# Reordering two places of a one-layer encoder kernel: two high halves on ScalarE, and the last products of the MLP

## The chip, the cores and the metric

The kernel runs on one core of one Trainium2 chip. The metric is the device time of one execution in microseconds; the median of several executions is compared. A profiled execution gives one trace with the start and the length of every instruction.

## The reference

One layer on 512 positions of width 1024, all in float32: a combined input projection into forgetting attention and a gated linear recurrence, an output projection, cross attention to 256 memory tokens, and a squared-ReLU MLP of width 4096, each with a residual addition, then a final RMS norm.

```python
h = h + jnp.concatenate([fox_out, rec], axis=-1) @ w_out[l]
h = h + memory_cross_attention(rmsnorm(h, norm_x_g[l]), mem_n, w_xq[l], w_xkv[l], w_xo[l])
u = rmsnorm(h, norm_ff_g[l]) @ w1[l]
h = h + jnp.square(jax.nn.relu(u)) @ w2[l]
...
return rmsnorm(h, final_norm_g)
```

The change touches the last three of these lines: the start of `@ w1`, the end of `@ w2`, and the final norm with the store of the output.

## The kernel before

**Numbers in two halves.** Every float32 operand of a matrix product is split in a high half, rounded on ScalarE (ACT) by an `activation` with `Copy`, and a low half, the difference, made on VectorE (DVE). A product is three matmuls: high by high, high by low, low by high. `split_of` makes the halves of a weight tile (L179 the high one, L183 the low one; tiles `whu`, `wlu` for the first MLP matrix, `whd`, `wld` for the second). `whp` and `wlp`, the pools of weight halves, have four buffers each.

**Seven products.** Each MLP product of 2 by 2 blocks is done with seven block products instead of eight, named "1" to "7", on sums and differences of blocks. The hidden width is cut into eight groups of 512 (`NG` is 8). For each group `mlp_up7` does the seven products with the first matrix (L1473 to L1475), into PSUM banks U, V and Y, and `mlp_down` the seven with the second (L1629 to L1631). The last two groups, 6 and 7, are taken through `mlp_down` together, as one pair: each product runs over both groups and over two row halves `t`, in four blocks of six matmuls, accumulated in one PSUM bank for each `t`.

**Queues.** PE's order is the program's. On ACT and DVE a scheduler orders the instructions by priority and by its own clock, except within `tc.manual_schedule`, where their order among themselves is as written. All engines run their queues in order. A dependency with `NoSync` is an order on one engine alone.

**Ahead of the first group.** The last column chunk of the cross attention's output projection (`xw`, L253 to L255) is still on PE when ACT and DVE prepare the operands of the first group within a manual stretch (from L1798). `x_hi_of(n)` writes the high half `xs_hi` of the moving operand of product n (L1538), `x_lo_of(n)` the low half `xs_lo` (L1549 for product 6, L1551 for others), `x_dif` their source `xd` (L1523), `x_scaled` scales a chunk (`xg`, L1508), and `split_first("6", "h")` and `("6", "l")` are the two halves of product 6's weights. The tile `xs_hi` and the weight buffer that product 6's high half gets by rotation were both last read by L254.

**The closing pair.** `PRODUCTS` gives the order 1, 5, 6, 2, 7, 3, 4. `hidden_part` makes the two halves `hb` of the hidden operand (L1576 on ACT, L1580 and L1582 on DVE), some products ahead. `add_to` (L1595, L1597) adds a finished bank to rows of the accumulator: `acc[0..3]` are four blocks of 128 positions by 1024 columns, with the residual in them. Product 7 ends the right half of blocks 2 and 3, product 2 the left and product 3 the right half of blocks 0 and 1, product 4 the left half of blocks 2 and 3. `finish` does, when the first half of a block is done, its sum of squares `fe` (ACT, then POOL, L1749 and L1750) and its product with the gain, `fa` (POOL, L1752); for the second half of blocks 0 and 1 it only notes the block in `deferred`. After product 7, `onto_rows` adds the accumulator's left halves of blocks 2 and 3 and bank U together (L1654 to L1657), so that product 4 accumulates onto them.

`last_product` does product 4 in three parts: row half 0 in bank U (`u0`, L1672), then the left and the right quarter of row half 1 (`z0`, `z1`). Between and behind them stand, in written order, the sums of squares, the row scales (`row_scale`, a power on POOL, L1720), the two scalings of each block (`scale_a` on ACT, L1728, of the half already multiplied by the gain; `scale_b` on DVE, L1737) and the stores to the output (L1694, L1701, L1712 and L1732). Blocks 0 and 1 have their squares, scalings and stores within product 4. The scaling `scale_a` of block 2 stands behind the square of `z1` on ACT.

Of the kernel before, what the change touches and what calls it, by code (L numbers as in the profile page):

```python
# [13 lines left out]
ALU = mybir.AluOpType  # L14
# [32 lines left out]
def emit(  # L47
# [49 lines left out]
    def s4(shape, name, dt=F32):  # L97
        return s4p.tile([P] + shape, dt, tag="s4", name=name)
# [18 lines left out]
    def mm(name, shape=(S,)):  # L117
        return mmp.tile([P] + list(shape), F32, tag="mm", name=name)
# [10 lines left out]
    def f(a):  # L129
        return a.bitcast(F32)  # L130
# [1184 lines left out]
    sqs, comb, hbs = {}, {}, {}  # L1315
    PRODUCTS = ("1", "5", "6", "2", "7", "3", "4")
    SPLITS = ("1", "6", "5", "2", "7", "3", "4")
    FIRST = ("1", "2", "5", "6", "7", "3", "4")
    QUAD = {"1": "00", "2": "10", "3": "11"}
    raw_n = [0]  # L1320
# [96 lines left out]
            add_unit(("u", g, part), [UK, WT])  # L1417

    def down_units(gs):
        for name in PRODUCTS:  # L1420
            for g in gs:
                add_unit(("d", g, name), [2, S])

# [137 lines left out]
        comb[g] = {"1": A1a, "5": s5, "6": n6, "3": s3, "7": s7, "2": A1b, "4": A2b}  # L1561

    hb_order = [(g, name) for g in range(NG - 2) for name in PRODUCTS]
    hb_order += [(g, name) for name in PRODUCTS for g in (NG - 2, NG - 1)]
    hb_used = [0]

    def behind_w4(at, n):
        order_only = mybir.DependencyInfo(mybir.DependencyClass.NoSync, mybir.DependencyReason.DATA)
# [2 lines left out]
    def hidden_part(g, name):  # L1571

        src = comb[g][name]
        hb = s4([2, 2, HS], f"hb{g}{name}", R)
        sign = -1.0 if name == "6" else 1.0
        at = ac.activation(hb[:, 0], src, AF.Copy, scale=sign)  # L1576
        if g == 0 and name == "1":
            behind_w4(at, 0)
        if name == "6":
            ve.scalar_tensor_tensor(hb[:, 1], src, -1.0, f(hb[:, 0]), op0=ALU.mult, op1=ALU.subtract)  # L1580
        else:
            ve.tensor_tensor(hb[:, 1], src, f(hb[:, 0]), ALU.subtract)  # L1582
        hbs[g, name] = hb

    def hidden_ahead(key, n, within=None):
# [6 lines left out]
    def add_to(ps, rows, half, t, sign):  # L1592
        a = acc[2 * rows + t][:, half * S : (half + 1) * S]
        if sign > 0:
            ve.tensor_tensor(a, ps, a, ALU.add)  # L1595
        else:
            ve.scalar_tensor_tensor(a, ps, -1.0, a, op0=ALU.mult, op1=ALU.add)  # L1597

    PLAN = {
        "1": ("U", True, ()),  # L1600
# [8 lines left out]
    def mlp_down(gs):  # L1609

        end = gs[-1] == NG - 1
        banks = {}
        for n, name in enumerate(PRODUCTS):
            bank, first_, goes = PLAN[name]
            if end and name == PRODUCTS[-1]:
                last_product(gs, banks)
                return
            for g, t in [(g, t) for g in gs for t in range(2)]:
                whi, wlo = unit("d", g, name)
                hidden_ahead((g, name), 1)  # L1620
                hb = hbs[g, name]
                if first_ and g == gs[0]:
                    banks[bank, t] = {"U": sc, "Y": tr}[bank](f"{bank}{g}{t}")
                ps = banks[bank, t]
                ts_ = slice(t * P, (t + 1) * P)
                for k in range(2):
                    hi, lo = hb[:, 0, k, ts_], hb[:, 1, k, ts_]
# [3 lines left out]
                    at = te.matmul(ps, lo, whi[:, k, :], start=False, stop=k == 1, skip_group_check=True)  # L1631
                presum.tick(6 * S / 2400, at)
                if end and (g, t) == (gs[0], 1):
                    hidden_ahead((g, name), HB + 1)
                if g != gs[-1]:
                    continue
                if name == "1":
                    banks["V", t] = mm(f"V{g}{t}")
                    ac.activation(banks["V", t], ps, AF.Copy)
                for rows, half, sign in goes:  # L1640
                    add_to(ps, rows, half, t, sign)
                    if end and (name, rows) in FINAL:
                        finish(2 * rows + t, half)
            if end and name == "7":
                onto_rows(banks)
            hidden_ahead((gs[-1], name), HB, gs)
            yield

    onto = []

    def onto_rows(banks):

        u0, u1, a = banks["U", 0], banks["U", 1], acc[3]
        ve.tensor_tensor(u0, u0, acc[2][:, 0:S], ALU.add)  # L1654
        onto.append(mm("Z1")[:, 0:HS])
        ve.tensor_tensor(onto[0], u1[:, HS:S], a[:, HS:S], ALU.add)
        ve.tensor_tensor(a[:, 0:HS], u1[:, 0:HS], a[:, 0:HS], ALU.add)  # L1657

    def last_product(gs, banks):

        name = PRODUCTS[-1]

        def steps(g, t, cols):
            (whi, wlo), hb = unit("d", g, name), hbs[g, name]
            for k in range(2):
                hi, lo = (hb[:, x, k, t * P : (t + 1) * P] for x in range(2))
                yield from ((hi, whi[:, k, cols]), (hi, wlo[:, k, cols]), (lo, whi[:, k, cols]))

        def product(ps, t, cols, start):
            ops = [op for g in gs for op in steps(g, t, cols)]  # L1670
            for i, (a, b) in enumerate(ops):
                te.matmul(ps, a, b, start=start and i == 0, stop=i == len(ops) - 1, skip_group_check=True)  # L1672

        with tc.manual_schedule(engines={mybir.EngineType.Activation, mybir.EngineType.DVE}):
            u0 = banks["U", 0]
            product(u0, 0, slice(0, S), False)
            o2, o3 = s4([D], "fo2"), s4([D], "fo3")
            (half, o0, r0_), (_, o1, r1_) = deferred
            hs = slice(half * S, (half + 1) * S)
            e0 = sm(1, "fv0")  # L1680
            ac.activation(o0[:, hs], acc[0][:, hs], AF.Square, scale=1.0 / 32.0, accum_out=e0)
            gp.tensor_tensor(e0, e0, fin[0][0], op=ALU.add)
            row_scale(r0_, e0)
            row_scale(r1_, squares(acc[1][:, hs], o1[:, hs], fin[1][0], "fv1"))
            e2, e3, r2_, r3_ = sm(1, "fv2"), sm(1, "fv3"), sm(1, "fr2"), sm(1, "fr3")
            scale_b(0, half, o0, r0_)
            ac.activation(o2[:, 0:S], u0, AF.Square, scale=1.0 / 32.0, accum_out=e2)
            gp.tensor_tensor(e2, e2, fin[2][0], op=ALU.add)
            row_scale(r2_, e2)
            scale_a(0, o0, r0_)  # L1690
            scale_a(1, o1, r1_)
            scale_b(1, half, o1, r1_)
            for tb, o in ((0, o0), (1, o1)):
                nc.sync.dma_start(out[rows_(tb), :], o)  # L1694
            h0, h1 = slice(0, HS), slice(HS, S)
            z0, z1 = mm("Z0")[:, 0:HS], onto[0]
            product(z0, 1, h0, True)
            ve.tensor_tensor(acc[3][:, h0], z0, acc[3][:, h0], ALU.add)
            v3 = squares(acc[3][:, h0], o3[:, h0], fin[3][0], "fv30")
# [3 lines left out]
            ac.activation(o3[:, h1], z1, AF.Square, scale=1.0 / 32.0, accum_out=e3)  # L1703
            scale_a(2, o2, r2_)
            dma_a(nc.sync, 2, o2)
            ve.tensor_tensor(e3, e3, v3, ALU.add)
            row_scale(r3_, e3)
            scale_a(3, o3, r3_)
            dma_a(ac, 3, o3)
            for cs, src in ((h0, acc[3][:, h0]), (h1, z1)):  # L1710
                ve.scalar_tensor_tensor(o3[:, cs], src, r3_, gfin[0][:, cs], op0=ALU.mult, op1=ALU.mult)
            nc.sync.dma_start(out[rows_(3), 0:S], o3[:, 0:S])  # L1712

# [5 lines left out]
    def row_scale(r, v):  # L1719
        gp.tensor_tensor(r, v, mhalf[:, 0:1], op=ALU.pow)  # L1720
        return r
# [12 lines left out]
    def scale_b(tb, half, o, r, src=None):  # L1734
        cs = slice(half * S, (half + 1) * S)
        src = acc[tb][:, cs] if src is None else src
        ve.scalar_tensor_tensor(o[:, cs], src, r, gfin[half], op0=ALU.mult, op1=ALU.mult)  # L1737


    FINAL = (("2", 0), ("7", 1), ("3", 0))  # L1740
# [2 lines left out]
    def finish(tb, half):  # L1743
# [3 lines left out]
        if tb not in fin:  # L1747
# [4 lines left out]
            gp.tensor_tensor(ag, a[:, cs], gfin[half], op=ALU.mult)  # L1752
            fin[tb] = (e, cs, ag)
            return
        o, r = s4([D], f"fo{tb}"), sm(1, f"fr{tb}")
        deferred.append((half, o, r))

    for part in FIRST:
# [146 lines left out]
```

## Time and profile before

| | us |
|---|---|
| median of 3 runs | 753.86 (753.45 to 754.28) |
| profiled execution, its time | 753.76 |
| its span, first instruction to last | 751.8 |
| PE busy / weight loads / DVE / ACT / POOL | 743.0 / 652.7 / 544.6 / 440.7 / 202.3 |
| mean granted TensorE clock | 0.998 of full speed |
| the first MLP group starts on PE | 430.02 |
| the pair's product 7 starts | 728.85 |
| product 3 starts | 734.29 |
| product 4 starts | 739.73 |
| last matmul starts | 745.21 |

A row of a timeline has the start from the span's first instruction, the length, engine, line and operation, the tiles written and read with their sizes, the count of instructions merged into it, and in brackets how long the engine had been idle before and what ended that. A row of waits has who waited, for whom, the total in us, the times and the longest.

### The profile page before, as it was taken

Reading aid. Unit: us, or ns where it says so; the run is one execution under the profiler, and the core shown is the slowest. Engines: PE = TensorE matmul, PEld = TensorE weight load, DVE = VectorE, ACT = ScalarE, POOL = GpSimd, SP = SyncE. Lnnn points to the kernel's source line nnn. Section 1 sums busy time; section 2 is a strip of 40 time slices with the busy share of each in tenths; the row PEclk is TensorE's granted clock in tenths of the full one; section 3 lists DMA queues with packets and bytes.
Section 4 is the critical chain, followed back from the end, with each engine's and each line's share of the span. In section 5 each row is a group of like instructions: output and inputs, shape, how many; then the busy total and the mean of one; then the engine's idle time right before and its main releaser. Section 6 shows DMA issues by size and latency. Waiting matters only on the chain.

```text
span 751.8 us, 12385 instructions
## 1 busy us (share of the span) xinstructions
PE 743.0 (99%) x4645; PEld 652.7 (87%) x4645; DVE 544.6 (72%) x859; ACT 440.7 (59%) x735; POOL 202.3 (27%) x279
## 2 busy tenths in 40 slices
PE   9999999999999999999999999999999999999996
PEld 6889888888888988888888899898989899999985
DVE  5647873677878756645555799978787887878796
ACT  5655555655666532334434589766566757574863
POOL 7207531233433227621111212111111111100034
PEclk9999999999999999999999999999999999999999
DMA  8641987567957789986578799998989898977452
GB/s 249 200 116 58 307 263 224 182 223 258 294 183 224 261 223 210 196 165 123 121 168 191 118 246 230 245 218 243 239 219 233 221 252 212 243 190 231 134 112 112
DMA packets 109677, 152.92 MB, mean 203 GB/s; under 512 B 6145, under 2 KB 75818, under 8 KB 109618
## 3 DMA queue, kind: packets, MB, share of 16 engines
q1 hardware_dynamic: 85458, 112.52, 45.9%
q0 software_dynamic: 24000, 39.35, 30.3%
q8 instruction: 36, 0.59, 0.3%
q10 hardware_dynamic: 160, 0.27, 0.1%
q14 instruction: 23, 0.19, 0.1%
HBM read 147.91 MB, written 51.40 MB: 265 GB/s over the span
## 4 chain that ended last, share of the span: by engine, by line
PE 91%; DVE 4%; ACT 2%; issue 1%; POOL 1%; DMA 1%; POOLq 0%; SPq 0%; DVEq 0%; ACTq 0%
PE uU L1474 4%; PE uU L1475 4%; PE uU L1473 4%; PE U L1629 3%; PE U L1630 3%; PE U L1631 3%; PE xq L253 2%; PE wo L253 2%; PE xq L254 2%; PE xq L255 2%; PE xw L253 2%; PE xw L254 2%; PE wo L255 2%; PE wo L254 2%; PE uY L1475 2%; PE uY L1474 2%
## 5 line engine op out<-in xcount | busy, mean ns | idle before, releaser
L183 DVE TENSOR_TENSOR wlu<-wru,whu 128x1024 fp32r<-128x1024 f32 x53 | 64.0, 1226 | 26.3 <-ACT whu L179 26.2
L179 ACT ACTIVATE whu<-wru 128x1024 fp32r<-128x1024 f32 x53 | 55.7, 1058 | 41.2 <-PE U L1631 16.8
L183 DVE TENSOR_TENSOR wld<-wrd,whd 128x1024 fp32r<-128x1024 f32 x56 | 69.1, 1236 | 13.8 <-ACT whd L179 13.6
L179 ACT ACTIVATE whd<-wrd 128x1024 fp32r<-128x1024 f32 x56 | 59.0, 1053 | 14.0 <-PE uU L1474 6.3
L1629 PE MATMUL U<-whd,hb 128*128 128x512 f32 x120 | 46.8, 390 | 0.0
L1630 PE MATMUL U<-wld,hb 128*128 128x512 f32 x120 | 46.8, 390 | 0.0
L1631 PE MATMUL U<-whd,hb 128*128 128x512 f32 x120 | 46.7, 389 | 0.0
L1014 POOL TENSOR_SCALAR bi<-nF,Ft 128x128 f32<-128x128 f32 (+3 forms) x32 | 20.8, 656 | 60.4 <-PE pt L1046 33.8
L1474 PE MATMUL uU<-xs_lo,whu 128*128 128x256 f32 x128 | 36.3, 284 | 0.2 <-DVE xs_lo L1549 0.2
L1473 PE MATMUL uU<-xs_hi,whu 128*128 128x256 f32 x128 | 36.3, 284 | 0.0
L1475 PE MATMUL uU<-x_hi,wlu 128*128 128x256 f32 x128 | 36.2, 283 | 0.0
L1473 PE MATMUL uY<-xs_hi,whu 128*128 128x256 f32 x128 | 36.2, 283 | 0.0
L1474 PE MATMUL uY<-xs_lo,whu 128*128 128x256 f32 x128 | 36.2, 283 | 0.0
L1475 PE MATMUL uY<-xs_hi,wlu 128*128 128x256 f32 x128 | 36.2, 283 | 0.0
L1474 PE MATMUL uU<-x_lo,whu 128*128 128x256 f32 x128 | 36.2, 283 | 0.0
L1475 PE MATMUL uU<-xs_hi,wlu 128*128 128x256 f32 x128 | 36.2, 283 | 0.0
L1473 PE MATMUL uU<-x_hi,whu 128*128 128x256 f32 x128 | 36.2, 283 | 0.0
L444 POOL DMA_DIRECT2D wsd<-in_w_dram x16 | 17.8, 1116 | 63.7 <-PE xw L255 12.8
L1369 POOL DMA_DIRECT2D wrd<-in_w_dram x8 | 9.8, 1220 | 86.9 <-DVE wld L183 76.4
L444 POOL DMA_DIRECT2D wsu<-in_w_dram x14 | 17.1, 1220 | 48.2 <-PE xw L255 15.6
L1631 PEld LDWEIGHTS U<-whd,hb 128*128 128x128 f32 x120 | 22.5, 188 | 4.8
L1629 PEld LDWEIGHTS U<-whd,hb 128*128 128x128 f32 x120 | 22.6, 188 | 4.5
(958 smaller groups left out, 2621.2 us busy)
## 6 DMA issues: line engine op xcount, KB each, us to landing
wru<-in_w_dram SPq DMA_DIRECT2D x25, 512.0 KB, 8.0
wsd<-in_w_dram SPq DMA_DIRECT2D x24, 512.0 KB, 7.0
wrd<-in_w_dram SPq DMA_DIRECT2D x24, 512.0 KB, 4.4
wrd<-wsd SPq DMA_DIRECT2D x24, 512.0 KB, 6.0
wsu<-in_w_dram SPq DMA_DIRECT2D x21, 512.0 KB, 6.8
wru<-wsu SPq DMA_DIRECT2D x21, 512.0 KB, 5.8
wsd<-in_w_dram POOLq DMA_DIRECT2D x16, 512.0 KB, 6.6
wsu<-in_w_dram POOLq DMA_DIRECT2D x14, 512.0 KB, 7.1
```

The source lines that it names most:

```text
L179: at = ac.activation(hi, raw, AF.Copy)
L183: at_lo = ve.tensor_tensor(lo, raw, f(hi), ALU.subtract)
L253: te.matmul(ps, wh, hi, start=n_ == 0 and not begun, stop=False)
L254: te.matmul(ps, wh, lo, start=False, stop=False)
L255: at = te.matmul(ps, wl, hi, start=False, stop=k == order[-1])
L444: yield gp.dma_start(wsum[kind, g, name], src, accum_op=ALU.add, **more)
L1473: te.matmul(ps[:, i, :], whi[:, k, ws], xh[:, k, :], start=begin, stop=False, skip_group_check=True)
L1474: te.matmul(ps[:, i, :], whi[:, k, ws], xl[:, k, :], start=False, stop=False, skip_group_check=True)
L1475: at = te.matmul(ps[:, i, :], wlo[:, k, ws], xh[:, k, :], start=False, stop=k == UK - 1, skip_group_check=True)
L1629: te.matmul(ps, hi, whi[:, k, :], start=begin, stop=False, skip_group_check=True)
L1630: te.matmul(ps, hi, wlo[:, k, :], start=False, stop=False, skip_group_check=True)
L1631: at = te.matmul(ps, lo, whi[:, k, :], start=False, stop=k == 1, skip_group_check=True)
```

## The change

In the manual stretch ahead of the first group, `split_first("6", "h")` is placed ahead of `x_hi_of("5", slice(0, 2))`. Both write a high half on ACT.

In the closing pair the order is `CLOSING`: 1, 5, 6, 2, 3, 7, 4. Loads, splits and hidden halves follow it. Product 7 runs its four blocks with the row half outermost: both groups for row half 0, then both for row half 1. When row half 0 is done, its addition to the accumulator is ordered on DVE behind the last low half of a hidden operand, and bank `u0` gets its accumulator rows at once; `onto_rows` is gone, and its other two additions stand in `last_product`. `finish` squares the second half of blocks 0 and 1 on ACT and makes their row scales on POOL itself. Their scalings and stores are written at the head of `last_product`, ahead of product 4's instructions, and the DVE ones are ordered behind the addition to `u0`. `scale_a` of block 2 and its store are written ahead of the square of `z1`.

```diff
+    CLOSING = ("1", "5", "6", "2", "3", "7", "4")
...
-        for name in PRODUCTS:
+        for name in CLOSING if gs[-1] == NG - 1 else PRODUCTS:
...
-    hb_order += [(g, name) for name in PRODUCTS for g in (NG - 2, NG - 1)]
+    hb_order += [(g, name) for name in CLOSING for g in (NG - 2, NG - 1)]
...
-            ve.tensor_tensor(hb[:, 1], src, f(hb[:, 0]), ALU.subtract)
+            at_lo[0] = ve.tensor_tensor(hb[:, 1], src, f(hb[:, 0]), ALU.subtract)
...
-            for g, t in [(g, t) for g in gs for t in range(2)]:
+            rows_first = end and name == "7"
+            for g, t in [(g, t) for t in range(2) for g in gs] if rows_first else [(g, t) for g in gs for t in range(2)]:
...
-                if end and (g, t) == (gs[0], 1):
+                if end and (g, t) == ((gs[1], 0) if rows_first else (gs[0], 1)):
                     hidden_ahead((g, name), HB + 1)
...
-                    add_to(ps, rows, half, t, sign)
+                    at = add_to(ps, rows, half, t, sign)
+                    if rows_first and t == 0:
+                        order_only = mybir.DependencyInfo(mybir.DependencyClass.NoSync, mybir.DependencyReason.DATA)
+                        tc.add_manual_dep(at.ins, at_lo[0].ins.name, order_only, reason="last low half first")
+                        at_u0.append(ve.tensor_tensor(ps, ps, acc[2][:, 0:S], ALU.add))
...
-            if end and name == "7":
-                onto_rows(banks)
...
-            u0 = banks["U", 0]
+            u0, u1, a = banks["U", 0], banks["U", 1], acc[3]
...
+            for tb, (half, o, r_) in enumerate(deferred):
+                scale_a(tb, o, r_)
+                at = scale_b(tb, half, o, r_)
...
+                tc.add_manual_dep(at.ins, at_u0[0].ins.name, order_only, reason="product 4 first")
+                nc.sync.dma_start(out[rows_(tb), :], o)
+            ve.tensor_tensor(z1, u1[:, h1], a[:, h1], ALU.add)
+            ve.tensor_tensor(a[:, h0], u1[:, h0], a[:, h0], ALU.add)
             product(u0, 0, slice(0, S), False)
-            e0 = sm(1, "fv0")
-            ac.activation(o0[:, hs], acc[0][:, hs], AF.Square, scale=1.0 / 32.0, accum_out=e0)
-            gp.tensor_tensor(e0, e0, fin[0][0], op=ALU.add)
-            row_scale(r0_, e0)
-            row_scale(r1_, squares(acc[1][:, hs], o1[:, hs], fin[1][0], "fv1"))
-            scale_b(0, half, o0, r0_)
             ac.activation(o2[:, 0:S], u0, AF.Square, scale=1.0 / 32.0, accum_out=e2)
             gp.tensor_tensor(e2, e2, fin[2][0], op=ALU.add)
             row_scale(r2_, e2)
-            scale_a(0, o0, r0_)
-            scale_a(1, o1, r1_)
-            scale_b(1, half, o1, r1_)
-            for tb, o in ((0, o0), (1, o1)):
-                nc.sync.dma_start(out[rows_(tb), :], o)
+            scale_a(2, o2, r2_)
+            dma_a(nc.sync, 2, o2)
             product(z0, 1, h0, True)
...
             ac.activation(o3[:, h1], z1, AF.Square, scale=1.0 / 32.0, accum_out=e3)
-            scale_a(2, o2, r2_)
-            dma_a(nc.sync, 2, o2)
...
-        o, r = s4([D], f"fo{tb}"), sm(1, f"fr{tb}")
+        o, r, e = s4([D], f"fo{tb}"), sm(1, f"fr{tb}"), sm(1, f"fv{tb}")
+        ac.activation(o[:, cs], a[:, cs], AF.Square, scale=1.0 / 32.0, accum_out=e)
+        gp.tensor_tensor(e, e, fin[tb][0], op=ALU.add)
+        row_scale(r, e)
...
+        split_first("6", "h")
         x_hi_of("5", slice(0, 2))
-        split_first("6", "h")
```

More of the change, by code (lines that the diff above doesn't have):

```diff
@@ L1563, in emit @@
     hb_order = [(g, name) for g in range(NG - 2) for name in PRODUCTS]
-    hb_order += [(g, name) for name in PRODUCTS for g in (NG - 2, NG - 1)]
+    hb_order += [(g, name) for name in CLOSING for g in (NG - 2, NG - 1)]
     hb_used = [0]
+    at_lo = [None]
     def behind_w4(at, n):
@@ L1594, in add_to @@
         if sign > 0:
-            ve.tensor_tensor(a, ps, a, ALU.add)
-        else:
-            ve.scalar_tensor_tensor(a, ps, -1.0, a, op0=ALU.mult, op1=ALU.add)
+            return ve.tensor_tensor(a, ps, a, ALU.add)
+        return ve.scalar_tensor_tensor(a, ps, -1.0, a, op0=ALU.mult, op1=ALU.add)
     PLAN = {
@@ L1612, in mlp_down @@
         banks = {}
-        for n, name in enumerate(PRODUCTS):
+        for name in CLOSING if end else PRODUCTS:
             bank, first_, goes = PLAN[name]
-            if end and name == PRODUCTS[-1]:
+            if end and name == CLOSING[-1]:
                 last_product(gs, banks)
                 return
-            for g, t in [(g, t) for g in gs for t in range(2)]:
+            rows_first = end and name == "7"
+            for g, t in [(g, t) for t in range(2) for g in gs] if rows_first else [(g, t) for g in gs for t in range(2)]:
                 whi, wlo = unit("d", g, name)
@@ L1640, in mlp_down @@
                 for rows, half, sign in goes:
-                    add_to(ps, rows, half, t, sign)
+                    at = add_to(ps, rows, half, t, sign)
[3 more added lines that the diff above has]
+                        at_u0.append(ve.tensor_tensor(ps, ps, acc[2][:, 0:S], ALU.add))
                     if end and (name, rows) in FINAL:
                         finish(2 * rows + t, half)
-            if end and name == "7":
-                onto_rows(banks)
             hidden_ahead((gs[-1], name), HB, gs)
             yield
[L1649 to L1657, printed above, removed]
+    at_u0 = []
     def last_product(gs, banks):
-        name = PRODUCTS[-1]
+        name = CLOSING[-1]
         def steps(g, t, cols):
@@ L1674, in last_product @@
         with tc.manual_schedule(engines={mybir.EngineType.Activation, mybir.EngineType.DVE}):
-            u0 = banks["U", 0]
-            product(u0, 0, slice(0, S), False)
-            o2, o3 = s4([D], "fo2"), s4([D], "fo3")
-            (half, o0, r0_), (_, o1, r1_) = deferred
-            hs = slice(half * S, (half + 1) * S)
-            e0 = sm(1, "fv0")
-            ac.activation(o0[:, hs], acc[0][:, hs], AF.Square, scale=1.0 / 32.0, accum_out=e0)
-            gp.tensor_tensor(e0, e0, fin[0][0], op=ALU.add)
-            row_scale(r0_, e0)
-            row_scale(r1_, squares(acc[1][:, hs], o1[:, hs], fin[1][0], "fv1"))
-            e2, e3, r2_, r3_ = sm(1, "fv2"), sm(1, "fv3"), sm(1, "fr2"), sm(1, "fr3")
-            scale_b(0, half, o0, r0_)
+            u0, u1, a = banks["U", 0], banks["U", 1], acc[3]
+            o2, o3 = s4([D], "fo2"), s4([D], "fo3")
+            e2, e3, r2_, r3_ = sm(1, "fv2"), sm(1, "fv3"), sm(1, "fr2"), sm(1, "fr3")
+            h0, h1 = slice(0, HS), slice(HS, S)
+            z0, z1 = mm("Z0")[:, 0:HS], mm("Z1")[:, 0:HS]
+            for tb, (half, o, r_) in enumerate(deferred):
+                scale_a(tb, o, r_)
+                at = scale_b(tb, half, o, r_)
+                order_only = mybir.DependencyInfo(mybir.DependencyClass.NoSync, mybir.DependencyReason.DATA)
+                tc.add_manual_dep(at.ins, at_u0[0].ins.name, order_only, reason="product 4 first")
+                nc.sync.dma_start(out[rows_(tb), :], o)
+            ve.tensor_tensor(z1, u1[:, h1], a[:, h1], ALU.add)
+            ve.tensor_tensor(a[:, h0], u1[:, h0], a[:, h0], ALU.add)
+            product(u0, 0, slice(0, S), False)
             ac.activation(o2[:, 0:S], u0, AF.Square, scale=1.0 / 32.0, accum_out=e2)
@@ L1689, in last_product @@
             row_scale(r2_, e2)
-            scale_a(0, o0, r0_)
-            scale_a(1, o1, r1_)
-            scale_b(1, half, o1, r1_)
-            for tb, o in ((0, o0), (1, o1)):
-                nc.sync.dma_start(out[rows_(tb), :], o)
-            h0, h1 = slice(0, HS), slice(HS, S)
-            z0, z1 = mm("Z0")[:, 0:HS], onto[0]
+            scale_a(2, o2, r2_)
+            dma_a(nc.sync, 2, o2)
             product(z0, 1, h0, True)
-            ve.tensor_tensor(acc[3][:, h0], z0, acc[3][:, h0], ALU.add)
-            v3 = squares(acc[3][:, h0], o3[:, h0], fin[3][0], "fv30")
+            ve.tensor_tensor(a[:, h0], z0, a[:, h0], ALU.add)
+            v3 = squares(a[:, h0], o3[:, h0], fin[3][0], "fv30")
             scale_b(2, 0, o2, r2_, u0)
@@ L1709, in last_product @@
             dma_a(ac, 3, o3)
-            for cs, src in ((h0, acc[3][:, h0]), (h1, z1)):
+            for cs, src in ((h0, a[:, h0]), (h1, z1)):
                 ve.scalar_tensor_tensor(o3[:, cs], src, r3_, gfin[0][:, cs], op0=ALU.mult, op1=ALU.mult)
@@ L1736, in scale_b @@
         src = acc[tb][:, cs] if src is None else src
-        ve.scalar_tensor_tensor(o[:, cs], src, r, gfin[half], op0=ALU.mult, op1=ALU.mult)
+        return ve.scalar_tensor_tensor(o[:, cs], src, r, gfin[half], op0=ALU.mult, op1=ALU.mult)
     FINAL = (("2", 0), ("7", 1), ("3", 0))
```

## The prediction

> **What bounds the kernel now.** I read the page first: engine shares, then the chain that ended last.
>
> ```profile
> span 751.8 us, 12385 instructions
> PE 743.0 (99%) x4645; PEld 652.7 (87%) x4645; DVE 544.6 (72%) x859; ACT 440.7 (59%) x735; POOL 202.3 (27%) x279
> PE 91%; DVE 4%; ACT 2%; issue 1%; POOL 1%; DMA 1%; POOLq 0%; SPq 0%; DVEq 0%; ACTq 0%
> ```
>
> TensorE is busy 99% of the span. No matmul is removed, so time can only come out of its waits or out of what follows its last matmul. The view of waits, for PE alone, gives the first:
>
> ```profile
> ...
> PE pt L1046 <- DVE bi L1038: 0.7, 1, 0.7
> PE uU L1474 <- DVE xs_lo L1549: 0.2, 1, 0.2
> ```
>
> The one left out and the L1046 row belong to stages far ahead of every edit. The L1474 row lies near one: product 6 of the first MLP group waits for the low half of its moving operand. It is worth more than 0.2 us, as the timeline of the weight loads shows (start, length, in brackets the idle time before it):
>
> ```profile
> 438.42 0.19 PEld L1475 LDWEIGHTS uY<-xs_hi,wlu 128*128 128x128 f32 x1
> 438.54 0.19 PEld L1473 LDWEIGHTS uU<-xs_hi,whu 128*128 128x128 f32 x1
> 439.17 0.19 PEld L1474 LDWEIGHTS uU<-xs_lo,whu 128*128 128x128 f32 x1 [0.44 <-DVE xs_lo L1549]
> ```
>
> Loads come every 0.12 us; this one was due at 438.66 and started at 439.17, so the stall is 0.51 us. From there on no PE wait is listed, so whatever is saved here arrives at the last matmul, unless the closing pair spoils it. The tail, from the timelines of PE, ACT, SP and the table by stretches (the columns after the stretch are PE, PEld, DVE, ACT, POOL, clock, DMA share, GB/s):
>
> ```profile
> 745.21 0.28 PE L1672 MATMUL Z<-whd,hb 128*128 128x256 f32 x1
> 745.58 0.38 ACT L1703 ACTIVATE fo<-Z 128x256 f32<-128x256 f32 x1 [1.02 <-PE Z L1672]
> 745.96 0.71 ACT L1728 ACTIVATE fo<-fa,fr 128x512 f32<-128x512 f32 x1
> 743.98 0.97 SPq L1694 DMA_DIRECT2D out_dram<-fo  x2
> 747.66 0.42 ACTq L1732 DMA_DIRECT2D out_dram<-fo  x1
> 747.81 0.33 SPq L1712 DMA_DIRECT2D out_dram<-fo  x1
> 744.75:745.00 0.25, 0.25 (x5) 0.25 (x4) 0.25 (x1) 0.00 (x0) 0.00 (x0) 1.00 0.69 279
> 747.00:748.00 1.00, 0.00 (x0) 0.00 (x0) 0.79 (x2) 0.63 (x1) 0.00 (x0) 1.00 0.99 383
> 750.00:750.25 0.25, 0.00 (x0) 0.00 (x0) 0.00 (x0) 0.00 (x0) 0.00 (x0) 0.50 0.89 311
> ```
>
> The last matmul ends at 745.49; its square, the row scale, the last scaling and two DMA issues follow one another to 747.81. The DMA engines work at 383 GB/s without a break from about 744.83 to 750.25. So the end is set by PE, then a serial chain, then a DMA queue that is still full.
>
> **First edit: the exchange on ScalarE.** The stall's chain, ACT then DVE, in a stretch whose order on both engines is pinned:
>
> ```profile
> 429.99 0.63 ACT L1538 ACTIVATE xs_hi<-xd 128x512 fp32r<-128x512 f32 x1 [1.50 <-PE xw L254]
> 430.53 1.05 ACT L179 ACTIVATE whu<-wr 128x1024 fp32r<-128x1024 f32 x1
> 431.48 0.71 ACT L1508 ACTIVATE xg<-hT,gv 128x512 f32<-128x512 f32 x1
> ...
> 431.61 1.23 DVE L183 TENSOR_TENSOR wlu<-wr,whu 128x1024 fp32r<-128x1024 f32 x1 [0.70 <-ACT whu L179]
> 432.75 0.75 DVE L1523 TENSOR_TENSOR xd<-xg,hT 128x256 f32<-128x256 f32 x2
> ...
> 436.79 1.06 ACT L1538 ACTIVATE xs_hi<-xd 128x1024 fp32r<-128x1024 f32 x1 [0.24 <-DVE xd L1523]
> ...
> 437.89 1.23 DVE L1549 SCALAR_TENSOR_TENSOR xs_lo<-xd,xs_hi 128x1024 fp32r<-128x1024 f32 x1 [0.53 <-ACT xs_hi L1538]
> ```
>
> DVE idles 0.70 us until `split_first("6","h")` has written whu. Put ahead of `x_hi_of("5", 0:2)`, that split takes its start at 429.99: what held ACT was the output projection's last L254 matmul, which reads both the o_lo tile and the weight buffer that the rotation of four gives to whu, so neither instruction can go earlier by being first. It then ends at 431.05 instead of 431.58, and the low split starts near 431.08, 0.53 us earlier. xg, third in the queue, still starts at 431.48 and ends at 432.19, just before xd wants it at 432.22. From xd on each step waits for the one before, on DVE or ACT (the idle 0.24 and 0.53 above), so x_lo of product 6 ends at 438.59 instead of 439.12. The load due at 438.66 finds it there with a few hundredths to spare. The delayed xs_hi of product 5 ends at 431.58; its readers come behind the xd pair of 432.75, after 433.5. **Term: −0.5 us** (ends: 0 if a link not seen here holds the chain, −0.51 because the stall is no longer).
>
> **Second edit: product 3 ahead of 7.** Both are 24 matmuls, so PE's sum doesn't change. Loads, splits and hidden halves of the two swap places one for one; the queues of SP and POOL keep their number of loads, and the last split, whd at 734.49, waited for a buffer and PE, not for a load. Cost 0. With the rows-first order the second group's share of 7 is wanted after one block of six matmuls instead of two; its low split, the wld of 732.82 below, was done at 734.0. Matmuls of this product follow one another every 0.227 us (seven steps from 739.73 to 741.32), so it is wanted at 739.73 − 17 × 0.227 = 735.9. Cost 0.
>
> What moves on DVE is riskier, and its rows are these (timeline of DVE, POOL, ACT, PE in the closing pair):
>
> ```profile
> 729.34 3.00 POOL L1752 TENSOR_TENSOR fa<-acc,gfin 128x512 f32<-128x512 f32 x2 [10.80 <-DVE acc L1595]
> 729.77 1.42 DVE L1582 TENSOR_TENSOR hb<-s,hb 128x512 fp32r<-128x512 f32 x1
> 732.82 1.21 DVE L183 TENSOR_TENSOR wld<-wrd,whd 128x1024 fp32r<-128x1024 f32 x1
> 733.95 0.68 DVE L1582 TENSOR_TENSOR hb<-sq,hb 128x512 fp32r<-128x512 f32 x1
> 734.49 1.07 ACT L179 ACTIVATE whd<-wrd 128x1024 fp32r<-128x1024 f32 x1 [1.52 <-PE U L1631]
> 735.69 1.28 DVE L1597 SCALAR_TENSOR_TENSOR acc<-U,acc 128x512 f32<-128x512 f32 x2
> 736.45 2.55 POOL L1752 TENSOR_TENSOR fa<-acc,gfin 128x512 f32<-128x512 f32 x2 [2.37 <-DVE acc L1597]
> 736.89 0.68 DVE L1654 TENSOR_TENSOR U<-U,acc 128x512 f32<-128x512 f32 x1
> 738.15 1.93 DVE L183 TENSOR_TENSOR wld<-wrd,whd 128x1024 fp32r<-128x1024 f32 x1
> 738.95 1.32 POOL L1750 TENSOR_TENSOR fe<-fe,eps 128x1 f32<-128x1 f32 x2
> 739.73 0.39 PE L1672 MATMUL U<-whd,hb 128*128 128x512 f32 x1
> 741.32 0.39 PE L1672 MATMUL U<-wld,hb 128*128 128x512 f32 x1
> 742.92 1.42 DVE L1737 SCALAR_TENSOR_TENSOR fo<-acc,fr,gfin 128x512 f32<-128x512 f32 x2 [0.73 <-POOL fr L1720]
> 743.42 0.30 POOL L1688 TENSOR_TENSOR fv<-fv,fe 128x1 f32<-128x1 f32 x1
> 743.80 0.93 POOL L1720 TENSOR_TENSOR fr<-fv,mhalf 128x1 f32<-128x1 f32 x1
> 746.33 0.54 POOL L1720 TENSOR_TENSOR fr<-fv,mhalf 128x1 f32<-128x1 f32 x1 [1.60 <-DVE fv L1706]
> ```
>
> Now the first addition into U bank 0 (L1654) is done by 737.57, two us ahead of product 4's first matmul at 739.73. After the change it needs product 7's first two blocks, ready at 739.73 − 12 × 0.227 + 0.16 = 737.2, where 0.16 is what a matmul's 0.39 outlasts its step. DVE in my order: the pair of product 3's row additions in the slots of 735.69, to 736.9; the last wld (its whd is there from 735.6), to 738.1; product 7's first addition 0.64, to 738.7; U bank 0's, to 739.3. Slack to 739.73 less the load's 0.11: 0.3 us. The wait on the last low half costs nothing, as those are through by 734.6. **Term: 0** (ends 0 to +0.3, should that wld run as slowly as the 1.93 one).
>
> Behind it on DVE: the final scalings of blocks 0 and 1 (0.71 each by the L1737 row, up to 1.42 beside fa), product 7's second addition, the two half-width additions of rows 3. That is 3.0 to 4.1 us from 739.3, over by 742.3 to 743.4; the last z product starts twelve steps of 0.12 before the last matmul's successor would, at 743.9. Cost 0. The DVE square of block 1 goes to ACT, which idles there.
>
> There the trace shows something that speaks against the new place. An hb low half takes 1.42 us beside POOL's fa product and 0.68 clear of it (733.95); L1654, with one operand in PSUM, keeps 0.68 beside fa. The Trainium skill, "SBUF — State Buffer", section "SBUF: two separate sides", says that a GpSimd operation and a DVE operation with two SBUF inputs exclude one another for the whole instruction. The trace agrees on which operations suffer. After the change it is the final scalings (two SBUF inputs) that meet the fa products of rows 2 and 3; the bound of 1.42 above holds that.
>
> **Third edit: `scale_a(2)` ahead of the last square on ACT.** Before, it ran at 745.96, behind the square and ahead of nothing urgent. Now the square of z1 (745.58) queues behind it, and it waits for r2 from POOL, which was ready at 743.80 + 0.93 = 744.73. At 0.71 it would end at 745.44: the square is not late. But POOL now has fa and fe of row 3 in front of r2: fa starts when product 7's second addition is done, near 742.0; 1.28 to 1.50 for it, about 0.66 for fe, 0.30 for the sum, 0.54 to 0.93 for the power puts r2 at 744.8 to 745.4. **Term: taken 0**, because the low end leaves the square on time; ends 0 to +0.5.
>
> **Fourth: the emptier DMA queue.** Blocks 0 and 1 (two of 512 KB) leave about three us earlier. The last SP issue at 747.81 would, by the first one's 0.85 us from issue to data (743.98 to 744.83, as the stretch from 744.75 is 0.69 busy), move data from 748.66; two last pieces of 256 KB at 383 GB/s take 1.37, to 750.03 instead of 750.25. **Term: −0.2 us** (ends 0 and −0.25, the backlog at 748.66).
>
> The Trainium skill, "DMA: Bandwidth & Descriptors", section "Anatomy of one DMA", gives 2.0 us plus bytes over 436 GB/s for a lone DMA. As an estimate by that page, 256 KB issued at 747.81 would land at 750.41, and the term would be −0.4; no row here shows a lone output.
>
> **Sum.** −0.5 + 0 + 0 − 0.2 = −0.7 us. The profiled execution took 753.76 us (span 751.8 and 2.0 around it) and lies 0.1 below the median 753.86; the sum gives 753.1 for a profile and **753.2** as the median.
>
> **Rivals.** (1) *Tail queue*: r2 is late and holds the last square by 0.2 to 0.5; the L1703 row then starts that much behind PE. 753.4 to 753.7. For it: POOL's longer queue; against: the rough spans of POOL. (2) *The exchange gives nothing*, because the margin of a few hundredths fails or ACT's order brings a new wait; only the drain remains, 753.7. (3) *Slower*: the last wld is put behind the two final scalings on DVE. Its place is before the matmul at 741.32. From 738.5 two scalings at 1.42 end at 741.3, and the wld of 1.93 at 743.3: PE stands 2.0 us, total 753.9 + 2.0 − 0.7 = 755.2. It decides once that wld ends after 741.9, where the stall eats the gain of 0.7. Against: that wld is ready from 735.6 and DVE has nothing else until 737.2. (4) *Lone DMA*: the drain is worth 0.4 and the margin holds, 753.0.
>
> **Chances.** Forecast 0.45, (1) 0.22, (2) 0.15, (3) 0.08, (4) 0.10. The three runs of before lie between 753.45 and 754.28, so the median itself is uncertain by some 0.3. Range: 752.5 (the largest gain, 0.9, and noise) to 754.3 (rival 1 or 2 and noise); only rival 3 and stray values are out. 0.2% is 1.5 us, about what a measurement of this kernel can tell from no change. No case reaches −1.5: faster 0.06 for what I have not seen. Slower, rival 3 and something like it: 0.09. Same: 0.85.
>
> **What would show it.** Right: whu at L179 starts near 429.99 and xs_hi after it; the PE row of waits for xs_lo gone or under 0.1; the last matmul near 744.7; L1654's successor done before product 4; DMA share falling to zero between 743 and 745 and the last data near 749.5. Wrong: a PE wait on U, Z or wld after 734; the last square starting over 0.2 us behind the last matmul; an unchanged gap from last matmul to span end (6.3 us) would refute the drain term.

## The result and the profile after

| | before | after |
|---|---|---|
| median, 22 runs each | 754.05 us (753.39 to 754.42) | 752.78 us (752.36 to 753.35) |
| ratio | | 0.9984, 95% interval 0.9979 to 0.9990 |
| profiled execution | 753.76 | 752.66 |
| its span | 751.8 | 750.9 |
| around the span | 2.0 | 1.75 |

The changed kernel is faster by 0.16%, 1.2 us. That is inside the forecast range and under the 0.2% that the prediction called "same"; the forecast gain was 0.7 us. The page first: PE's work is the same 743.0 us. DMA is gone from the chain that ended last, but that row says little: the control below, with the stores in their old place, has no DMA in it either.

```profile
span 750.9 us, 12388 instructions
PE 743.0 (99%) x4645; PEld 653.4 (87%) x4645; DVE 543.0 (72%) x857; ACT 441.6 (59%) x737; POOL 203.2 (27%) x280
PE 92%; DVE 2%; ACT 2%; issue 2%; POOL 1%; POOLq 0%; DVEq 0%; ACTq 0%
```

All waits of PE. The one for `xs_lo` has left the list:

```profile
PE warm L365 <- DVE ones L369: 1.3, 1, 1.3
PE pt L1046 <- DVE bi L1038: 0.7, 1, 0.7
```

The chain that the exchange shortens, from the timelines of ACT, DVE and the weight loads (lines have moved by one, L1474 is now L1475):

```profile
429.94 1.06 ACT L179 ACTIVATE whu<-wr 128x1024 fp32r<-128x1024 f32 x1 [1.50 <-PE xw L254]
430.91 0.62 ACT L1539 ACTIVATE xs_hi<-xd 128x512 fp32r<-128x512 f32 x1
431.04 1.23 DVE L183 TENSOR_TENSOR wlu<-wr,whu 128x1024 fp32r<-128x1024 f32 x1 [0.18 <-ACT whu L179]
437.31 1.23 DVE L1550 SCALAR_TENSOR_TENSOR xs_lo<-xd,xs_hi 128x1024 fp32r<-128x1024 f32 x1 [0.52 <-ACT xs_hi L1539]
438.48 0.19 PEld L1474 LDWEIGHTS uU<-xs_hi,whu 128*128 128x128 f32 x1
438.60 0.19 PEld L1475 LDWEIGHTS uU<-xs_lo,whu 128*128 128x128 f32 x1
```

The split waits for L254 in the place of `xs_hi`, DVE's idle 0.70 shrinks to 0.18, `xs_lo` ends at 438.54, and the load comes on the beat at 438.60, 0.06 us later.

The closing pair, from the timelines of DVE, POOL, ACT, PE and its loads:

```profile
735.74 1.21 DVE L183 TENSOR_TENSOR wld<-wrd,whd 128x1024 fp32r<-128x1024 f32 x1
737.15 0.69 DVE L1585 TENSOR_TENSOR hb<-sq,hb 128x512 fp32r<-128x512 f32 x1 [0.20 <-ACT hb L1579]
737.76 0.68 DVE L1599 SCALAR_TENSOR_TENSOR acc<-U,acc 128x512 f32<-128x512 f32 x1
738.37 0.69 DVE L1648 TENSOR_TENSOR U<-U,acc 128x512 f32<-128x512 f32 x1
738.53 1.29 POOL L1744 TENSOR_TENSOR fa<-acc,gfin 128x512 f32<-128x512 f32 x1
738.75 0.19 PEld L1634 LDWEIGHTS U<-whd,hb 128*128 128x128 f32 x1
738.96 1.41 DVE L1729 SCALAR_TENSOR_TENSOR fo<-acc,fr,gfin 128x512 f32<-128x512 f32 x1
739.17 0.19 PEld L1669 LDWEIGHTS U<-whd,hb 128*128 128x128 f32 x1 [0.23 <-issue]
740.29 0.68 DVE L1599 SCALAR_TENSOR_TENSOR acc<-U,acc 128x512 f32<-128x512 f32 x1
741.05 1.74 POOL L1744 TENSOR_TENSOR fa<-acc,gfin 128x512 f32<-128x512 f32 x1 [0.63 <-DVE acc L1599]
743.31 0.54 POOL L1712 TENSOR_TENSOR fr<-fv,mhalf 128x1 f32<-128x1 f32 x1
743.88 0.72 ACT L1720 ACTIVATE fo<-fa,fr 128x512 f32<-128x512 f32 x1 [0.98 <-POOL fr L1712]
744.77 0.28 PE L1669 MATMUL Z<-whd,hb 128*128 128x256 f32 x1
745.14 0.38 ACT L1697 ACTIVATE fo<-Z 128x256 f32<-128x256 f32 x1 [0.54 <-PE Z L1669]
```

Here something was lost. Bank U's addition (L1648) ends at 739.06. Loads come every 0.23 us here, so product 4's first load was due at 738.98, behind that of 738.75; it comes at 739.17.

The stores: the timeline of SP and ACT, the table by stretches (columns as in the prediction; the last two are the DMA share and GB/s), and the stores of 256 KB in the view of DMA issues, whose last column is the time from issue to landing, before and after:

```profile
740.45 1.60 SPq L1682 DMA_DIRECT2D out_dram<-fo  x2
747.22 0.42 ACTq L1724 DMA_DIRECT2D out_dram<-fo  x1
747.37 0.33 SPq L1704 DMA_DIRECT2D out_dram<-fo  x1
747.50:748.00 0.50, 0.00 (x0) 0.00 (x0) 0.00 (x0) 0.00 (x0) 0.00 (x0) 1.00 0.00 0
748.25:748.50 0.25, 0.00 (x0) 0.00 (x0) 0.00 (x0) 0.00 (x0) 0.00 (x0) 1.00 1.02 393
749.50:749.75 0.25, 0.00 (x0) 0.00 (x0) 0.00 (x0) 0.00 (x0) 0.00 (x0) 0.76 0.12 33
```

```profile
out_dram<-fo SPq DMA_DIRECT2D x3, 256.0 KB, 3.0
...
out_dram<-fo SPq DMA_DIRECT2D x3, 256.0 KB, 2.6
```

The DMA engines are idle when the last two stores arrive; the last one lands after 2.6 us instead of 3.0.

**One measure for all kernels.** In the profiles the first matmul of the MLP starts anywhere from 429.65 to 430.65 us, differences that arise almost wholly in the first 15 us of the kernel. All distances below are therefore taken within a profile: from that matmul to the last matmul's start and to the span's end, and from the last store's issue to the last landing. "Around" is the time minus the span, the mean over the runs.

| kernel | median | first MLP matmul to last | to span end | issue to landing | around |
|---|---|---|---|---|---|
| before | 754.05 | 315.19 | 321.73 | 3.03 | 2.0 |
| after | 752.78 | 314.80 | 320.94 | 2.62 | 1.75 |
| exchange alone | 753.05 | 314.69 | 321.31 | 3.10 | 1.72 |
| closing pair alone | 753.38 | 315.32 | 321.47 | 2.62 | 1.79 |
| late stores | 753.33 | 314.81 | 321.31 | 2.98 | 1.76 |
| no stores of 0, 1 | 753.69 | 315.20 | 321.46 | 2.62 | 2.02 |
| scaling of block 2 back | 752.84 | 314.80 | 320.96 | 2.63 | 1.77 |
| no "low half first" | 752.78 | 314.71 | 320.85 | 2.62 | 1.75 |
| split last store | 752.99 | 314.78 | 321.13 | 2.38 | 1.76 |
| control | 753.80 | 315.17 | 321.55 | 2.86 | 2.01 |
| both improvements | 752.34 | 314.71 | 320.61 | 2.35 | 1.75 |
| after, once more | 752.91 | 314.78 | 320.93 | 2.62 | 1.74 |

Medians of the kernel before, measured beside them, lay between 753.90 and 754.13. From before to after the table gives −0.39 to the last matmul, −0.41 from issue to landing, −0.25 around the span, together −1.05 of the 1.2; the rest has no place in the table.

The medians alone do not tell the kernel without the two stores (ratio to the kernel before 0.9996, interval 0.9987 to 1.0005) or the control (0.9997, 0.9988 to 1.0006) from the kernel before, nor the variants "scaling back", "no low half first" and "split last store" (0.9985 to 0.9986, intervals within 0.9976 to 0.9995) from the changed kernel. What is said of these below rests on one profile of each.

### The profile page after: what moved, and what is told of

Read it like the earlier page. It is cut to its first block, busy times and chain, and to the rows that moved or that the text cites. A ratio compares the mean times of both kernels' runs of the same rounds, so it can differ in the third digit from the quotient of the medians.

```text
span 750.9 us, 12388 instructions
## 1 busy us (share of the span) xinstructions
PE 743.0 (99%) x4645; PEld 653.4 (87%) x4645; DVE 543.0 (72%) x857; ACT 441.6 (59%) x737; POOL 203.2 (27%) x280
## 4 chain that ended last, share of the span: by engine, by line
PE 92%; DVE 2%; ACT 2%; issue 2%; POOL 1%; POOLq 0%; DVEq 0%; ACTq 0%
PE uU L1474 4%; PE uU L1476 4%; PE uU L1475 4%; PE U L1633 3%; PE U L1632 3%; PE U L1634 3%; PE uY L1474 2%; PE uY L1475 2%; PE uY L1476 2%; PE xq L253 2%; PE wo L253 2%; PE xq L254 2%; PE xw L254 2%; PE xw L253 2%; PE xq L255 2%; PE xw L255 2%
## 5 line engine op out<-in xcount | busy, mean ns | idle before, releaser
L1474 PE MATMUL uU<-xs_hi,whu 128*128 128x256 f32 x128 | 36.4, 284 | 0.0
L1474 PE MATMUL uY<-xs_hi,whu 128*128 128x256 f32 x128 | 36.3, 284 | 0.0
L1475 PE MATMUL uY<-xs_lo,whu 128*128 128x256 f32 x128 | 36.3, 284 | 0.0
L1475 PE MATMUL uU<-x_lo,whu 128*128 128x256 f32 x128 | 36.3, 284 | 0.0
L1475 PE MATMUL uU<-xs_lo,whu 128*128 128x256 f32 x128 | 36.3, 283 | 0.0
L1474 PE MATMUL uU<-x_hi,whu 128*128 128x256 f32 x128 | 36.2, 283 | 0.0
```

The lines of the kernel that those rows point to most:

```text
L1474: te.matmul(ps[:, i, :], whi[:, k, ws], xh[:, k, :], start=begin, stop=False, skip_group_check=True)
L1475: te.matmul(ps[:, i, :], whi[:, k, ws], xl[:, k, :], start=False, stop=False, skip_group_check=True)
```

## The experiments

**The exchange alone, on the kernel before.**

```diff
+        split_first("6", "h")
         x_hi_of("5", slice(0, 2))
-        split_first("6", "h")
```

> The kernel before with the exchange on ScalarE alone. My theory: the weight load that was due at 438.66 and started at 439.17 comes on time, so the last matmul starts 0.5 us earlier (744.7) and the span is 751.3; the tail is as before, 3.0 us from the last store's issue to its landing; time 0.5 under the kernel before. Rival (the gain of the whole change is made at the end alone): time as before.

Ratio 0.9989 (0.998 to 0.9997). The first theory holds: the PE wait is gone, the last matmul starts at 744.72, 0.50 us nearer to the first, and the last store takes as long as before. The medians differ by 0.85, more than expected. Of this 0.42 lies between the first MLP matmul and the span's end, and about 0.3 around the span, for which the theory has no place.

```profile
744.72 0.28 PE L1672 MATMUL Z<-whd,hb 128*128 128x256 f32 x1
out_dram<-fo SPq DMA_DIRECT2D x3, 256.0 KB, 3.1
```

**The closing pair alone: the changed kernel with the exchange undone.**

```diff
+        x_hi_of("5", slice(0, 2))
         split_first("6", "h")
-        x_hi_of("5", slice(0, 2))
```

> The changed kernel with the exchange undone. My theory: the PE wait of 439.17 is back, the last matmul starts 0.1 us later than in the kernel before (the small loss at product 4's start), the last store lands 2.6 us after its issue instead of 3.0, so the time is 0.3 to 0.4 under the kernel before. Rival (the end is worth the full 1.2 us of the medians): 1.2 under.

Ratio 0.9991 (0.9982 to 1.0). The stall is back, as the timeline of the loads shows, PE loses 0.13 us at the end, and the landing is the short one. The medians differ by 0.52, a little over the 0.3 to 0.4 expected, and here too the time around the span is 0.2 shorter. The end is not worth 1.2 us.

```profile
438.31 0.19 PEld L1474 LDWEIGHTS uU<-xs_hi,whu 128*128 128x128 f32 x1
438.94 0.19 PEld L1475 LDWEIGHTS uU<-xs_lo,whu 128*128 128x128 f32 x1 [0.44 <-DVE xs_lo L1550]
```

**Late stores: in the changed kernel the stores of blocks 0 and 1 wait for the last matmul of `z0`.**

```diff
-                nc.sync.dma_start(out[rows_(tb), :], o)
...
-            dma_a(nc.sync, 2, o2)
-            product(z0, 1, h0, True)
+            at_z0 = product(z0, 1, h0, True)
+            for tb, (half, o, r_) in enumerate(deferred):
+                dma = nc.sync.dma_start(out[rows_(tb), :], o)
+                sync = mybir.DependencyInfo(mybir.DependencyClass.Sync, mybir.DependencyReason.DATA)
+                tc.add_manual_dep(dma.ins, at_z0.ins.name, sync, reason="late stores")
+            tc.add_manual_dep(dma_a(nc.sync, 2, o2).ins, dma.ins.name, order_only, reason="late stores first")
```

> The changed kernel with the stores of blocks 0 and 1 held back until the left quarter of product 4 is done, about where the kernel before issues them. Theory 'full queue': the last store lands 3.0 us after its issue again, and 0.4 us of the gain is lost. Rival (the stores' place does not matter, the last landing is shorter for other reasons): 2.6 us, and the time of the changed kernel.

Ratio to the kernel before 0.9990 (0.9981 to 0.9999). The matmuls stay (314.81 to the last one), the landing is 2.98, and the span end moves by +0.37. From the last matmul's start to the span's end the kernel before has 6.54 us, the changed one 6.14, this one 6.50. The place of these two stores carries nearly the whole gain of the tail.

```profile
744.37 1.12 SPq L1692 DMA_DIRECT2D out_dram<-fo  x2
748.07 0.33 SPq L1708 DMA_DIRECT2D out_dram<-fo  x1
749.00:749.25 0.25, 0.00 (x0) 0.00 (x0) 0.00 (x0) 0.00 (x0) 0.00 (x0) 0.50 1.05 393
out_dram<-fo SPq DMA_DIRECT2D x3, 256.0 KB, 3.0
```

**The kernel before without these stores.**

```diff
-            for tb, o in ((0, o0), (1, o1)):
-                nc.sync.dma_start(out[rows_(tb), :], o)
```

> The kernel before without the stores of blocks 0 and 1 (these rows of the output are not written). Theory 'full queue': the last store lands 2.6 us after its issue, the span is 0.4 us shorter, all matmuls where they were. By my own backlog sum it would be 0.2. Rival: 3.0 us and no change.

All matmuls stay where they were, and the landing is 2.62. The span gains only 0.27 from the first MLP matmul on, not the 0.4 expected, because its end stands 1.03 us behind the landing here instead of 0.91, a point to which the split store comes back.

**The third edit undone.**

```diff
-            scale_a(2, o2, r2_)
-            dma_a(nc.sync, 2, o2)
             product(z0, 1, h0, True)
...
             ac.activation(o3[:, h1], z1, AF.Square, scale=1.0 / 32.0, accum_out=e3)
+            scale_a(2, o2, r2_)
+            dma_a(nc.sync, 2, o2)
```

> The changed kernel with the scaling and store of block 2's second half put back behind the last square on ScalarE. My theory (third edit worth 0): r2 is there 0.5 us before the square is due, so the square starts 0.37 us behind the last matmul in both, and so do both last stores; the time is that of the changed kernel within 0.1 us. Rival (ScalarE's queue in the tail matters, either way): the square or the last stores move by over 0.1 us.

Worth nothing: the square starts 0.38 us behind the last matmul's start here and 0.37 in the changed kernel, and the span end differs by 0.02.

```profile
745.19 0.38 ACT L1695 ACTIVATE fo<-Z 128x256 f32<-128x256 f32 x1 [2.24 <-PE Z L1669]
745.56 0.71 ACT L1720 ACTIVATE fo<-fa,fr 128x512 f32<-128x512 f32 x1
```

**Without "last low half first".**

```diff
-                        order_only = mybir.DependencyInfo(mybir.DependencyClass.NoSync, mybir.DependencyReason.DATA)
-                        tc.add_manual_dep(at.ins, at_lo[0].ins.name, order_only, reason="last low half first")
```

> The changed kernel without the order 'last low half first', so that product 7's first addition does not stand behind the last low half on VectorE; bank U's addition then ends about 0.3 us earlier, 738.8. Theory (the 0.1 us that PE loses at product 4's start is the wait for that addition): the load at 739.17 comes at 739.09 and the last matmul is 0.1 us earlier. Rival (the loss comes from the operand halves or the bank change): no difference.

Product 7's addition now precedes the low half. Bank U's addition ends at 738.55; this profile runs 0.22 us early, so that is 0.29 earlier than in the changed kernel. Product 4's load keeps the beat of 0.23, and the last matmul is 0.09 us nearer, although the low half itself now comes later. PE's small loss was the wait for this addition.

```profile
737.86 0.69 DVE L1646 TENSOR_TENSOR U<-U,acc 128x512 f32<-128x512 f32 x1
738.53 0.19 PEld L1634 LDWEIGHTS U<-whd,hb 128*128 128x128 f32 x1
738.76 0.19 PEld L1667 LDWEIGHTS U<-whd,hb 128*128 128x128 f32 x1
```

**The last store in two pieces.**

```diff
                 ve.scalar_tensor_tensor(o3[:, cs], src, r3_, gfin[0][:, cs], op0=ALU.mult, op1=ALU.mult)
-            nc.sync.dma_start(out[rows_(3), 0:S], o3[:, 0:S])
+                nc.sync.dma_start(out[rows_(3), cs], o3[:, cs])
```

> The changed kernel with the very last store cut in two of 128 KB, each issued behind its own scaling. Theory (the end is set by the last bytes on the DMA engines, then a fixed receipt): data start 0.3 to 0.4 us earlier and the span is 0.2 to 0.4 us shorter. Rival (a second issue and smaller pieces cost as much as they bring): no gain or a loss of 0.1 to 0.3.

Both were partly right. The last landing is 5.01 us behind the last matmul's start instead of 5.22, but the span end is 1.34 behind the landing instead of 0.92. In the trace SyncE checks the stores' semaphores one after another at the end, 0.06 us each. In the changed kernel the last store's is checked last; with one store more it is the first of the stores', and seven more follow after it has landed (750.00 to 750.43 in the trace). In the kernel without the two stores two checks follow behind the landing, 0.12 us, which is the 1.03 there instead of 0.91. The wait rows of SyncE for the stores show one long wait in the place of two (total, times, longest), the changed kernel first:

```profile
SPq L1895 <- DMA out_dram<-fo: 1.8, 2, 1.5
...
SPq L1895 <- DMA out_dram<-fo: 1.9, 1, 1.9
```

**The control: one idle instruction more in the kernel before.**

```diff
     scaling = scale_rows()
+    gp.memset(sm(1, "idle"), 0.0)
```

> The kernel before with one more instruction, a memset of a 128x1 tile on the mostly idle GpSimd engine ahead of the second MLP group. It does no work that anything waits for. Theory (the time outside the profiled span, 2.0 us in the kernel before and 1.75 in the changed one, goes with the build and not with the work): span as before, 751.4 to 752.5, time minus span anywhere from 1.7 to 2.0. Rival (it belongs to the work at the end): 2.0 as before.

The time around the span stayed 2.01, so it does not change with just any build. Every kernel with one of the two edits has 1.7 to 1.8. It does not go with the work at the end either: the exchange alone leaves that work as it was and has 1.72, and the kernel without the two stores has 2.02. What it consists of, no row shows; this stays open.

The control does the work of the kernel before, and its last store landed after 2.86 us, not 3.03. The tail of a single profile is known no better than that.

**Both improvements, and the changed kernel beside it.**

```diff
-                        order_only = mybir.DependencyInfo(mybir.DependencyClass.NoSync, mybir.DependencyReason.DATA)
-                        tc.add_manual_dep(at.ins, at_lo[0].ins.name, order_only, reason="last low half first")
...
-            dma_a(nc.sync, 2, o2)
...
-            nc.sync.dma_start(out[rows_(2), 0:S], o2[:, 0:S])
+            nc.sync.dma_start(out[rows_(2), :], o2)
...
-            nc.sync.dma_start(out[rows_(3), 0:S], o3[:, 0:S])
+                nc.sync.dma_start(out[rows_(3), cs], o3[:, cs])
```

> The changed kernel without the order 'last low half first', with the last store cut in two as in the run before, and block 2's two stores made one, so that the number of stores is again that of the changed kernel and the last store's semaphore is again the last that SyncE checks. Theory (the cut store landed 0.2 us earlier and lost 0.4 because its semaphore was checked first and eight others after it): last landing 5.0 us behind the last matmul instead of 5.2, span end 0.9 behind the landing, last matmul 0.1 earlier; 0.3 us under the changed kernel. Rival (the loss belongs to small pieces): the span end stays 1.3 behind the landing.

> The changed kernel once more, on the chip of the run it is compared with: 1.1 us under the kernel before, 0.8 of it in the span from the first MLP matmul on, the rest outside the span.

The span end is 0.91 behind the landing again, with the small pieces still there: the order of the checks was the loss. The landing takes 2.4 us.

```profile
out_dram<-fo SPq DMA_DIRECT2D x2, 128.0 KB, 2.4
SPq L1892 <- DMA out_dram<-fo: 1.5, 2, 1.2
```

Median 752.34 (752.02 to 753.08), ratio to the kernel before 0.9979 (0.997 to 0.9988). The changed kernel on the same chip had 752.91 (752.34 to 753.19), ratio 0.9983 (0.9974 to 0.9992). In the profiles this version is 0.32 us shorter from the first MLP matmul on than the changed kernel beside it. Its median is the lowest here, though the intervals of the two ratios overlap.

## Why the prediction was right, and where it was off

**The exchange, −0.5.** Right in place and size: 0.50 alone. The steps came as worked out: whu first, the low split 0.57 earlier in the row and 0.52 after taking off the 0.05 by which this profile runs early, and `xs_lo` a few hundredths before its load. Rival 2 falls with the first experiment.

**Product 3 ahead of 7, taken 0, ends 0 to +0.3.** It cost 0.09, inside the ends, by another step than I named. I had said that the wait on the last low half costs nothing, as those are through by 734.6. In the changed kernel that low half is no longer early. Its high half stands on ACT behind the two squares of blocks 0 and 1, which the change itself put there (735.26 to 736.50 on ACT, without a gap), and so the low half ran at 737.15, behind the wld. Bank U's addition ended at 739.06. In the time of the kernel before, where this stretch lies 0.53 us later (728.85 against 728.32 for the first matmul behind product 2), that is 739.6 instead of my 739.3. Taking the order away brought the addition back by 0.29 and the matmuls by 0.09, so the slack that I had put at 0.3 was 0.2. Rival 3 did not occur: the wld came ahead of the scalings.

**The scalings beside fa.** The first took 1.41 us, the second 0.73, where I had 0.71 to 1.42. The Trainium skill, "SBUF — State Buffer", section "SBUF: two separate sides", excludes a GpSimd operation and a DVE one with two SBUF inputs from each other; the trace agrees, since the addition with a PSUM operand that ran into fa (L1648) kept 0.69. Both scalings ran beside an fa. The first began behind it, at 738.96, and took 1.41 itself; the second began ahead of it, at 740.89, and there fa took 1.74 instead of 1.29. As `z1` was not yet due, it cost nothing.

**The third edit, 0, and rival 1.** Right. r2 was ready at 743.85, 1.29 us before the square, where my times had left 0.2 to 0.8. Product 7's second addition came at 740.29 and fa started at 741.05, which is 741.6 in the time of the kernel before, not near 742; from there to r2 it took 2.80 us, the low end of what I had added up.

**The drain, −0.2.** The step that failed in size. Between these two profiles it measured −0.41, and the gap that I had named as a sign, from the last matmul's end to the span's, fell from 6.3 to 5.9 us. The side after was right: the last store's data end 2.27 us after its issue, where I had 2.22. The side before was not. I had taken the data's end from the end of a stretch, 750.25; in the trace the last data packet of the stores ends at 750.37, and the next stretch still has some:

```profile
750.25:750.50 0.25, 0.00 (x0) 0.00 (x0) 0.00 (x0) 0.00 (x0) 0.00 (x0) 0.50 0.09 33
```

So the data give −0.29. The other 0.12 come behind the data, where I had assumed no change, and they do not belong to the full queue. From the end of the last data packet to the landing it is 0.35 to 0.37 us in ten of the twelve profiles, late stores and control among them; only the kernel before has 0.47 and the exchange alone 0.50. In these two a packet of the queue that the view of DMA calls `instruction` starts within 0.01 us of the end of the stores' last packet, at 750.38 and at 749.94. Whether it held the landing is not shown: without the two stores one ran from 749.65 to 750.34, across the landing, which came 0.35 behind the data all the same. What the full queue itself costs is the data's end: 2.51 to 2.63 us after the issue in the four kernels whose stores of blocks 0 and 1 leave late, 2.27 to 2.28 where the last store goes out whole on an empty queue, a term of about 0.23 to 0.36. The −0.41 is thus in part the chance of one profile.

Rival 4 had the size of −0.4. By the Trainium skill, "DMA: Bandwidth & Descriptors", section "Anatomy of one DMA — SWDGE (gpsimd) path", which gives its fit for DMAs issued by GpSimd, 2.0 us plus 256 KB at 436 GB/s make an estimate of 2.60. The trace has, for a store that SyncE issued, 2.62 once the engines are idle, and 2.86 to 3.10 in the kernels where they are not. That the two figures meet is no test of the fit: this store is not alone, as ACT issues another 256 KB 0.15 us ahead of it, at 747.22.

**Around the span.** I took the 2.0 us as constant. They fell by 0.25, with either edit alone; no step of the prediction covers it. Without these 0.25 and the 0.2 that the table does not place, the gain would be about 0.8, near the 0.7 forecast. But that sum too has a loss of 0.09 that I had put at 0 and a drain twice mine, so the nearness is in part luck.

## What to carry to other kernels

When one engine is busy 99% of the time, look for the single instruction that breaks its beat, and follow the idle brackets back to the first engine that could have run two ready instructions in the other order. At the end of a kernel the last store's landing counts: keep the DMA queue empty when it is issued, and see that its semaphore is the last one waited for. An order pinned on one engine should be checked again when the change delays the instruction that it waits for.

## What the runs showed that was not expected

The spread of one kernel's runs, about 1 us, need not hide a gain of 0.1: in the profiles the distance from the first MLP matmul to the last repeats to 0.03 us (315.17 to 315.20 in three profiles of kernels with the old order throughout, 314.78 to 314.81 in five with the new one), and the variation lies ahead of it. The tail behind the last matmul repeats less well while the DMA queue is full: 6.38 to 6.62 us in the four kernels whose stores of blocks 0 and 1 leave late. A store costs SyncE 0.06 us more at the end if its semaphore is checked behind the last landing. The time outside the profiled span differed by 0.25 us between kernels, stable within each; its cause is open.
